# A norm's weights moved from the rows to the raw up-projection weights, and a second weight load that waits for the last row norm

## The chip, the cores and the metric

One core of one Trainium2 chip runs the whole kernel. The metric is the device time of one execution in microseconds. A time is compared with a run of the kernel before on the same chip.

## What is computed

One layer of a decoder trunk on 1024 tokens of width 1024, in float32. The first half of the layer (a norm, one input projection, pooling heads and differential attention, one output projection with a residual add) is not touched. What matters is the second half, cut from the reference:

```
h  = rms_norm(x, norm_ffn_g[l], NORM_EPS)        # x * rsqrt(mean(x*x) + eps) * g, row by row
gu = h @ ffn_w_in[l]                             # 1024 -> 2 * 2816
g  = causal_depthwise_conv(gu[..., :D_FF], ffn_conv_w[l], ffn_conv_b[l])
u  = gu[..., D_FF:]
x  = x + (jax.nn.silu(g) * u) @ ffn_w_out[l]     # 2816 -> 1024
return rms_norm(x, norm_final_g, NORM_EPS)
```

## The kernel before, in words

Every product in float32 is made of three products of values split into a high part (a cast by ScalarE) and a low part (a subtraction by VectorE or GpSimd): L79 and L80 for weights, L83 and L84 for activations. TensorE (PE in the profile) is busy nearly throughout.

**The output projection and the second norm.** `out_rows` (L538 to L541) adds the last three groups of the output projection to the eight row tiles x1 of 128 tokens, tile by tile, two halves of 512 columns each. Behind each tile `norm2` squares the two halves on ScalarE (L566), stores the tile to memory (L568, on ScalarE's DMA queue), makes the reciprocal root with small steps on VectorE, ScalarE and VectorE (L570 to L576, and L108, L109, L111 of `newton`), and scales the tile with one VectorE instruction that multiplies by the row's factor and by the norm's weights g_ffn (L577). The tile is scaled where it lies, so L577 waits until the store of the unscaled tile has left.

**The blocks.** The up-projection is a fast 2x2 block product with seven products in place of eight. Its token operands are seven blocks: b11, b21 (the two halves of an even tile), b22 (the second half of an odd tile) and t1 to t4, sums of halves of an even and an odd tile made by `pair_blocks` (L594 to L597) on GpSimd, for the last pair partly on VectorE. Each piece is transposed on TensorE into PSUM (`to_block`, L584, tiles tp_b and tp_t) and split from there by ScalarE and VectorE into h and l. A product needs its block from all four pairs.

**The weights of a channel tile.** The 2816 channels are worked through in 22 tiles ct of 128 channels. `up_weights` loads the raw weights of the u half and the g half (ru, rg, 512 KB each; one buffer for each, so the next tile's load waits until both are used up), and makes four sums: s1 and s3 on GpSimd (L628, L631), s2 and s4 on VectorE (L629, L630; s1 and s2 are the halves of sa, s3 and s4 those of sb). Then u, sa, sb and a quarter of g (gt) are split: uh, ul, sah, sal, sbh, sbl. `ffn_up` runs seven products of 12 matmuls each (L650; 84 for a tile, 1848 in all) in the order 1 6 7 5 2 4 3, with steps between them that empty a bank: product 1 uses uh, ul and b11; product 6 sah, sal and t2; product 7 sbh, sbl and t3; product 5 sah, sal and t1; product 2 uh, ul and b21; product 4 gt and t4; product 3 sbh, sbl and b22. After product 5 ScalarE copies a bank into eb (L674), and products 3 and 4 can't start until that copy, and VectorE's add behind it (L675), are done.

**The order.** A scheduler fixes each engine's order when the kernel is built, mixing products of neighbouring channel tiles; on the chip every engine works through its own list in that order, and the head of a list blocks what is behind it. So the lists below are facts of the build, and only the times in them come from the chip.

Of the kernel before, what the change touches and what calls it, by code (L numbers as in the profile page):

```python
# [9 lines left out]
F32 = mybir.dt.float32  # L10
F32R = mybir.dt.float32r
AF = mybir.ActivationFunctionType
ALU = mybir.AluOpType
PSUM = bass.MemoryType.PSUM

P = 128
S = 1024
D = 1024
KC = D // P
NT = S // P  # L20
# [22 lines left out]
def trunk_kernel(ctx, tc, x, norm_mix_g, w_in, pool_w, rows, line, rel_bias, w_out, norm_ffn_g,  # L43
                 ffn_w_in, ffn_w_out, norm_final_g, onehot, out):
    nc = tc.nc
# [7 lines left out]
    const = ctx.enter_context(tc.tile_pool(name="const", bufs=1))  # L53
# [5 lines left out]
    att = st_att.enter_context(tc.tile_pool(name="att", bufs=1))  # L59
# [5 lines left out]
    def sc_ps(name):  # L65
        return ps_a.tile([P, 512], F32, tag="sc", bufs=3, name=name)

    def pv_ps(name):
        return ps_a.tile([P, 512], F32, tag="pv", bufs=1, name=name)
# [8 lines left out]
    def split(hi, lo, src, lo_eng=None):  # L78
        nc.scalar.copy(hi, src)  # L79
        (lo_eng or nc.gpsimd).tensor_tensor(lo, src, hi.bitcast(F32), op=ALU.subtract)  # L80
# [33 lines left out]
    def row_rstd(src, sq, name):  # L114
        ss = small.tile([P, 1], F32, tag="ss", name=f"ss_{name}")
        nc.scalar.activation(sq, src, AF.Square, accum_out=ss)
        var = small.tile([P, 1], F32, tag="var", name=f"var_{name}")
        nc.vector.tensor_scalar(var, ss, 1.0 / D, EPS, op0=ALU.mult, op1=ALU.add)
        r = small.tile([P, 1], F32, tag="rs", name=f"rs_{name}")
        lg = small.tile([P, 1], F32, tag="lg", name=f"lg_{name}")  # L120
        nc.scalar.activation(lg, var, AF.Ln)
        nc.scalar.activation(r, lg, AF.Exp, scale=-0.5)
        return newton(r, var, name)
# [25 lines left out]
    ident = const.tile([P, P], F32, name="ident")  # L149
# [20 lines left out]
        return xt  # L170


    prow = att.tile([96, P], F32, tag="ln", bufs=2, name="prow")
    flat = att.tile([P, 276], F32, tag="hank", bufs=1, name="flat")
    lam_in = flat[:, 0:256].rearrange("p (j c) -> p j c", c=64)
    recfar = const.tile([P, 20], F32, name="recfar")
# [4 lines left out]
    def load_params():  # L181
        nc.vector.memset(rb[32:33, :], NEG)
        nc.sync.dma_start(rb[0:32, :], rel_bias)
        nc.sync.dma_start(oh, onehot)
        nc.sync.dma_start(flat, line.to_broadcast((P, 276)))
        nc.sync.dma_start(prow[0:93, :], rows)

    prm = const.tile([P, 96], F32, name="prm")
    gsub = const.tile([P, 1], F32, name="gsub")
    nlam = const.tile([P, 1], F32, name="nlam")  # L190

    def small_params():
        r_ps = sc_ps("r_ps")
        nc.tensor.matmul(r_ps[0:NH, :], rb, oh, start=True, stop=True)
        r_sb = att.tile([NH, 512], F32, tag="vt", bufs=1, name="r_sb")
        nc.vector.tensor_copy(r_sb, r_ps[0:NH, :])
        nc.sync.dma_start(scratch, r_sb)
        prm_ps = sc_ps("prm_ps")
        nc.tensor.transpose(prm_ps[:, 0:93], prow[0:93, :], ident[0:93, 0:93])
        nc.vector.tensor_copy(prm[:, 0:93], prm_ps[:, 0:93])  # L200
        nc.vector.tensor_scalar(gsub, prm[:, 92:93], 1.0 - LAM_INIT, None, op0=ALU.mult)
        nc.vector.tensor_copy(recfar, flat[:, 256:276])
        lam_s = const.tile([P, 2], F32, name="lam_s")
        lam_p = att.tile([P, 64], F32, tag="tb", bufs=1, name="lam_p")
        for j in range(2):
            nc.vector.tensor_tensor_reduce(lam_p, lam_in[:, 2 * j, :], lam_in[:, 2 * j + 1, :], 1.0, 0.0,
                                           ALU.mult, ALU.add, lam_s[:, j:j + 1])
        lam_e = const.tile([P, 2], F32, name="lam_e")
        nc.scalar.activation(lam_e, lam_s, AF.Exp)
        nc.vector.tensor_tensor(nlam, lam_e[:, 1:2], lam_e[:, 0:1], op=ALU.subtract)  # L210
        nc.vector.tensor_scalar(nlam, nlam, -LAM_INIT, None, op0=ALU.add)
# [109 lines left out]
    for t in range(NT):  # L321
# [8 lines left out]
        xt = xs[t]  # L330
        sq = att.tile([P, S], F32, tag="pl", bufs=3, name=f"sq_{t}")
        r = row_rstd(xt, sq, f"m{t}")
# [184 lines left out]
    mid = ctx.enter_context(tc.tile_pool(name="mid", bufs=2, side="right"))  # L517

    def u_tile(dt, name):
        return wide.tile([P, S], dt, tag="u", name=name)  # L520

    def x_tile(dt, name):
        return wide.tile([P, S], dt, tag="x", bufs=4, name=name)
# [4 lines left out]
    x1 = [None] * NT  # L528
# [16 lines left out]
    for s in OUT_PLAN.split():  # L545
        if s[0] == "w":
            wo[int(s[1])] = out_weights(int(s[1]))
        else:
            out_rows(int(s[1]), wo[int(s[1])], int(s[2]))
    g_bc2 = mid.tile([P, D], F32, tag="gt", bufs=1, name="g_ffn")  # L550
    nc.sync.dma_start(g_bc2, norm_ffn_g.to_broadcast((P, D)))
    st_ws.close()
    st_slots.close()

# [6 lines left out]
    def norm2(t):  # L561
        xt = x1[t]
        ss = small.tile([P, 2], F32, tag="ss2", name=f"ssf_{t}")
        junk = pv_ps(f"junk_{t}")
        for half in range(2):
            nc.scalar.activation(junk, xt[:, half * 512:half * 512 + 512], AF.Square,  # L566
                                 accum_out=ss[:, half:half + 1])
        nc.scalar.dma_start(x1_d[t * P:(t + 1) * P, :], xt)  # L568
        var = small.tile([P, 1], F32, tag="var", name=f"varf_{t}")
        nc.vector.tensor_scalar(var, ss[:, 0:1], 1.0 / D, EPS, op0=ALU.mult, op1=ALU.add)  # L570
        nc.vector.tensor_scalar(var, ss[:, 1:2], 1.0 / D, var, op0=ALU.mult, op1=ALU.add)
        r = small.tile([P, 1], F32, tag="rs", name=f"rsf_{t}")
        lg = small.tile([P, 1], F32, tag="lg", name=f"lgf_{t}")
        nc.scalar.activation(lg, var, AF.Ln)
        nc.scalar.activation(r, lg, AF.Exp, scale=-0.5)
        r = newton(r, var, f"f{t}")  # L576
        nc.vector.scalar_tensor_tensor(xt, xt, r, g_bc2, op0=ALU.mult, op1=ALU.mult)  # L577

    def to_block(src, b, j):
        tp = (sc_ps if b[0] == "t" else tp_ps)(f"tp_{b}_{j}")  # L580
# [35 lines left out]
    def up_weights(ct):  # L616
        raw = []
        for n, c in (("u", NCT + ct), ("g", ct)):
            r = mid.tile([P, KC * P], F32, tag="rw", bufs=2, name=f"r{n}{ct}")
            src = ffn_w_in[:, c * P:(c + 1) * P].rearrange("(k p) c -> p k c", p=P)  # L620
            nc.sync.dma_start(r.rearrange("p (k c) -> p k c", c=P), src)
            raw.append(r)
        u, g = raw
        a11, a12, a21, a22 = u[:, 0:512], u[:, 512:1024], g[:, 0:512], g[:, 512:1024]
        sa = mid.tile([P, S], F32, tag="st", bufs=2, name=f"sa{ct}")
        sb = mid.tile([P, S], F32, tag="st", bufs=2, name=f"sb{ct}")
        s1, s2, s3, s4 = sa[:, 0:512], sa[:, 512:1024], sb[:, 0:512], sb[:, 512:1024]
        nc.gpsimd.tensor_tensor(s1, a21, a22, op=ALU.add)  # L628
        nc.vector.tensor_tensor(s2, s1, a11, op=ALU.subtract)  # L629
        nc.vector.tensor_tensor(s4, a12, s2, op=ALU.subtract)  # L630
        nc.gpsimd.tensor_tensor(s3, a11, a21, op=ALU.subtract)  # L631
        uh, ul = u_tile(F32R, f"uh{ct}"), u_tile(F32R, f"ul{ct}")
        split(uh, ul, u)
        gt = x_tile(F32R, f"gt{ct}")
        split(gt[:, 0:512], gt[:, 512:1024], a22, nc.vector)
        sh = []
        for n, t in (("a", sa), ("b", sb)):
            h, l = (u_tile if n == "a" else x_tile)(F32R, f"s{n}h{ct}"), u_tile(F32R, f"s{n}l{ct}")
            split(h, l, t, nc.vector)
            sh.append((blocks(h), blocks(l)))  # L640
        (ah, al), (bh_, bl_), (uh, ul), gb = sh[0], sh[1], (blocks(uh), blocks(ul)), blocks(gt)
        return {"1": (uh[:, 0], ul[:, 0], "b11"), "2": (uh[:, 1], ul[:, 1], "b21"), "3": (bh_[:, 1], bl_[:, 1], "b22"),
                "4": (gb[:, 0], gb[:, 1], "t4"), "5": (ah[:, 0], al[:, 0], "t1"), "6": (ah[:, 1], al[:, 1], "t2"),
                "7": (bh_[:, 0], bl_[:, 0], "t3")}
# [112 lines left out]
    ct = 0  # L757
    for gi, n in enumerate(DOWN):
        ops = []
        for c in range(ct, ct + n):  # L760
            rows = slice(c * P, (c + 1) * P)
# [31 lines left out]
def _arrays(a):  # L793
    import numpy as np
    onehot, rec = _tables()
    a = {n: np.asarray(v) for n, v in a.items()}
    rows = np.concatenate([a[n].reshape(-1, P) for n in ('ffn_conv_w', 'ffn_conv_b', 'pool_scale', 'subln_g')])
    line = np.concatenate([a[n].reshape(1, -1) for n in ('lambda_q1', 'lambda_k1', 'lambda_q2', 'lambda_k2')]
                          + [rec, a['rel_bias'][31:32]], axis=1)
    return [('x', a['x']), ('norm_mix_g', a['norm_mix_g']), ('w_in', a['w_in']), ('pool_w', a['pool_w']),  # L800
            ('rows', rows), ('line', line), ('rel_bias', a['rel_bias']), ('w_out', a['w_out']),
            ('norm_ffn_g', a['norm_ffn_g']), ('ffn_w_in', a['ffn_w_in']), ('ffn_w_out', a['ffn_w_out']),
            ('norm_final_g', a['norm_final_g']), ('onehot', onehot)]
# [22 lines left out]
```

## Time and profile before

| | |
|---|---|
| median of 3 runs | 1113.54 us (1113.4 to 1116.36) |
| the profiled execution's own time | 1115.49 us |
| its span in the trace | 1113.7 us |
| up-projection products, first to last start | 429.02 to some 866 us |
| mean granted TensorE clock, as a share of full speed | 0.987 |

The span is what the trace shows of the profiled execution; 1.8 us of its own time lie around it. Busy shares are averages over stages with different limits. The stage that the change touches is the passage from the output projection to the up-projection, at about 390 to 490 us, and the 22 channel tiles behind it, up to about 850 us.

### The profile page before, as it was taken

The numbers are of one execution on the slowest core, as the hardware profiler recorded it, in microseconds if no ns is written. First come the engines' busy times: TensorE is split into PE (matmuls) and PEld (weight loads), VectorE is DVE, ScalarE is ACT, GpSimd is POOL, SyncE is SP. The second block draws the span as 40 slices with busy tenths as digits, with TensorE's granted clock in tenths as the row PEclk, the third lists the DMA queues.
The fourth block names the chain that finished last, engine by engine and source line by source line (L and its number), as shares of the span: only waits on it lengthen the run. The fifth ranks groups of instructions, "written<-read, shape, count | busy, mean of one in ns | idle before, by whom it ended". The sixth has DMA issues, their size and how long they took to land.

```text
span 1113.7 us, 13597 instructions
## 1 busy us (share of the span) xinstructions
PE 1066.6 (96%) x5011; PEld 884.0 (79%) x5011; DVE 732.3 (66%) x1213; ACT 475.9 (43%) x775; POOL 341.7 (31%) x240
## 2 busy tenths in 40 slices
PE   5999999999899997999999999999999999999997
PEld 4988888887677675878888888888888788888885
DVE  7556787877797689577657656755665655544545
ACT  5557476655752355244333443443344222111133
POOL 3232242433730247133312232221314322221211
PEclk9999999999899998999999999999999999999999
DMA  8010110110386742123122212222247632212112
GB/s 242 28 50 27 43 46 19 43 39 26 133 278 216 242 171 76 57 95 95 57 94 95 93 59 96 90 81 76 82 127 267 223 114 99 89 60 95 39 50 102
DMA packets 85990, 111.76 MB, mean 100 GB/s; under 512 B 3618, under 2 KB 66303, under 8 KB 85924
## 3 DMA queue, kind: packets, MB, share of 16 engines
q1 hardware_dynamic: 79300, 86.78, 24.4%
q10 hardware_dynamic: 6624, 24.12, 5.5%
q8 instruction: 39, 0.64, 0.2%
q14 instruction: 27, 0.22, 0.1%
HBM read 82.57 MB, written 28.32 MB: 100 GB/s over the span
## 4 chain that ended last, share of the span: by engine, by line
PE 81%; DVE 8%; issue 4%; DMA 3%; ACT 1%; POOL 1%; SPq 1%; DVEq 0%; ACTq 0%; POOLq 0%
PE p L650 36%; PE fo L747 7%; PE fo L749 7%; PE fo L748 7%; PE tpa L402 1%; PE z_q L144 1%; PE z_q L145 1%; PE z_q L143 1%; PE o L538 1%; PE o L539 1%; PE o L540 1%; PE z_p L143 1%; PE z_p L144 1%; PE z_p L145 1%; PE z_v L143 1%
## 5 line engine op out<-in xcount | busy, mean ns | idle before, releaser
L747 PE MATMUL fo<-w,a 128*128 128x512 f32 x352 | 137.3, 390 | 2.8 <-DVE xr L750 2.8
L750 DVE TENSOR_TENSOR xr<-xr,fo 128x512 f32<-128x512 f32 x112 | 75.9, 684 | 97.0 <-PE fo L749 96.3
L748 PE MATMUL fo<-w,a 128*128 128x512 f32 x352 | 137.0, 389 | 0.0
L749 PE MATMUL fo<-w,a 128*128 128x512 f32 x352 | 137.0, 389 | 0.0
L80 POOL TENSOR_TENSOR w<-rw,w 128x1024 fp32r<-128x1024 f32 x22 | 61.3, 2796 | 156.4 <-ACT w L79 151.1
L628 POOL TENSOR_TENSOR sa<-rg 128x512 f32<-128x512 f32 x22 | 32.9, 1495 | 209.8 <-DMA rg<-in_ffn_w_in_dram 201.3
L80 POOL TENSOR_TENSOR ul<-ru,uh 128x1024 fp32r<-128x1024 f32 x22 | 58.1, 2642 | 71.8 <-PE p L650 37.6
L747 PEld LDWEIGHTS fo<-w,a 128*128 128x128 f32 x352 | 66.1, 188 | 17.6 <-DVE xr L750 4.0
L749 PEld LDWEIGHTS fo<-w,a 128*128 128x128 f32 x352 | 66.1, 188 | 13.9
L748 PEld LDWEIGHTS fo<-w,a 128*128 128x128 f32 x352 | 66.1, 188 | 13.6
L79 ACT CAST a<-ra 128x1024 fp32r<-128x1024 f32 x22 | 23.1, 1051 | 118.8 <-DVE xr L750 64.1
L362 ACT ACTIVATE p<-p,nm 128x128 f32<-128x128 f32 (+7 forms) x64 | 49.6, 776 | 40.9 <-DVE nm L361 40.5
L650 PE MATMUL p<-t4h,gt 128*128 128x512 f32 x176 | 58.9, 396 | 1.7 <-DVE g L675 1.7
L629 DVE TENSOR_TENSOR sa<-sa,ru 128x512 f32<-128x512 f32 x22 | 39.9, 1814 | 21.1 <-POOL sa L628 21.1
L538 PE MATMUL o<-woh,yh 128*128 128x512 f32 x128 | 51.9, 409 | 1.6 <-DVE x L541 1.4
L349 POOL CAST qz<-q 64x128 fp32r<-64x128 f32 x64 | 24.5, 384 | 92.3 <-PE s L353 85.4
L79 ACT CAST uh<-ru 128x1024 fp32r<-128x1024 f32 x22 | 23.2, 1054 | 68.0 <-PE p L650 67.4
L539 PE MATMUL o<-wol,yh 128*128 128x512 f32 x128 | 50.6, 397 | 1.4 <-POOL wol L80 1.4
L677 DVE TENSOR_TENSOR g<-eb,p 128x512 f32<-128x512 f32 x22 | 15.1, 687 | 55.5 <-PE p L650 55.5
L80 DVE TENSOR_TENSOR a<-ra,a 128x1024 fp32r<-128x1024 f32 x22 | 43.0, 1956 | 12.1 <-ACT a L79 11.6
L540 PE MATMUL o<-woh,yl 128*128 128x512 f32 x128 | 50.0, 393 | 0.9 <-DVE yl L80 0.9
L79 ACT CAST gt<-rg 128x512 fp32r<-128x512 f32 x22 | 13.7, 623 | 82.1 <-PE p L650 75.1
(264 smaller groups left out, 3111.0 us busy)
## 6 DMA issues: line engine op xcount, KB each, us to landing
x_rows<-x ACTq DMA_DIRECT2D x24, 512.0 KB, 3.6
ru<-in_ffn_w_in_dram SPq DMA_DIRECT2D x22, 512.0 KB, 4.0
rg<-in_ffn_w_in_dram SPq DMA_DIRECT2D x22, 512.0 KB, 3.9
act_rows<-cv ACTq DMA_DIRECT2D x22, 512.0 KB, 2.6
rw<-in_ffn_w_out_dram SPq DMA_DIRECT2D x22, 512.0 KB, 4.4
ra<-act_rows SPq DMA_DIRECT2D x22, 512.0 KB, 3.4
x<-in_x_dram SPq DMA_DIRECT2D x16, 512.0 KB, 5.6
x<-x_rows SPq DMA_DIRECT2D x16, 512.0 KB, 3.7
```

What stands on the lines that cost most here:

```text
L79: nc.scalar.copy(hi, src)
L80: (lo_eng or nc.gpsimd).tensor_tensor(lo, src, hi.bitcast(F32), op=ALU.subtract)
L362: nc.scalar.activation(s[:, 0:w], s[:, 0:w], AF.Exp, bias=negm[:, c:c + 1], accum_out=sums[:, c:c + 1])
L538: nc.tensor.matmul(ps, yh[:, ts], wh[:, cs], start=n == 0, stop=False)
L539: nc.tensor.matmul(ps, yh[:, ts], wl[:, cs], start=False, stop=False)
L540: nc.tensor.matmul(ps, yl[:, ts], wh[:, cs], start=False, stop=n == len(wo) - 1)
L629: nc.vector.tensor_tensor(s2, s1, a11, op=ALU.subtract)
L650: nc.tensor.matmul(ps, w[:, k, :], h[:, k, :], start=start and k == 0 and n == 0, stop=k == 3 and n == 2, skip_group_check=not start)
L747: nc.tensor.matmul(ps, ah[:, ts], wh[:, cs], start=n == 0, stop=False)
L748: nc.tensor.matmul(ps, ah[:, ts], wl[:, cs], start=False, stop=False)
L749: nc.tensor.matmul(ps, al[:, ts], wh[:, cs], start=False, stop=n == len(ops) - 1)
L750: nc.vector.tensor_tensor(xr[t][:, cs], xr[t][:, cs], ps, op=ALU.add)
```

## The change

The norm's weights norm_ffn_g are no longer multiplied into the rows. They arrive with the other small parameters (eight more rows of a table that is transposed once, so that prm[:, 93:101] holds the weight of input channel k*128+p in partition p, column k), and the broadcast load of g_ffn is gone. Two GpSimd instructions for each channel tile multiply the raw weights ru and rg by them, in place, before the sums. A row tile is scaled by its factor alone, on ScalarE. For channel tile 1 a one-column VectorE copy from the last scaled row tile writes into each raw buffer first, so that this tile's loads wait until the last row norm is done.

```
-    g_bc2 = mid.tile([P, D], F32, tag="gt", bufs=1, name="g_ffn")
-    nc.sync.dma_start(g_bc2, norm_ffn_g.to_broadcast((P, D)))
...
         r = newton(r, var, f"f{t}")
-        nc.vector.scalar_tensor_tensor(xt, xt, r, g_bc2, op0=ALU.mult, op1=ALU.mult)
+        nc.scalar.mul(xt, xt, r)
...
             r = mid.tile([P, KC * P], F32, tag="rw", bufs=2, name=f"r{n}{ct}")
+            if ct == 1:
+                nc.vector.tensor_copy(r[:, 0:1], x1[NT - 1][:, D - 1:D])
             src = ffn_w_in[:, c * P:(c + 1) * P].rearrange("(k p) c -> p k c", p=P)
             nc.sync.dma_start(r.rearrange("p (k c) -> p k c", c=P), src)
+            r3 = r.rearrange("p (k c) -> p k c", c=P)
+            nc.gpsimd.tensor_tensor(r3, r3, prm[:, 93:101].unsqueeze(2).to_broadcast((P, KC, P)), op=ALU.mult)
             raw.append(r)
```

The lines of the changed kernel stand two lower or two to three higher than those before: `pair_blocks` is L592 to L595, s1 to s4 are L630 to L633, the new multiplication is L623, the row scaling on ScalarE L575, the new copies L619, products L652.

**GpSimd, at the third pair of row tiles.** In these lists x1_2_5 is row tile 5, ta2 and tb2 hold the sums of pair 2, and the digit behind ru, rg, uh, ul, sa, sb is the channel tile. Before:

```order
L80 TENSOR_TENSOR ul0_4513<-ru0_4502,uh0_4512 128x1024
L628 TENSOR_TENSOR sa0_4506<-rg0_4504 128x512
L594 TENSOR_TENSOR ta2_4322<-x1_2_5_4280,x1_2_4_4224 128x512
L595 TENSOR_TENSOR tb2_4323<-x1_2_5_4280 128x512
L631 TENSOR_TENSOR sb0_4507<-ru0_4502,rg0_4504 128x512
L596 TENSOR_TENSOR ta2_4322<-x1_2_5_4280,ta2_4322 128x512
L597 TENSOR_TENSOR tb2_4323<-x1_2_4_4224,ta2_4322 128x512
L595 TENSOR_TENSOR tb3_4462<-x1_2_7_4419 128x512
```

and in the changed kernel:

```order
L592 TENSOR_TENSOR ta2_4320<-x1_2_5_4278,x1_2_4_4222 128x512
L593 TENSOR_TENSOR tb2_4321<-x1_2_5_4278 128x512
L594 TENSOR_TENSOR ta2_4320<-x1_2_5_4278,ta2_4320 128x512
L80 TENSOR_TENSOR ul0_4513<-ru0_4500,uh0_4512 128x1024
L630 TENSOR_TENSOR sa0_4506<-rg0_4503 128x512
L633 TENSOR_TENSOR sb0_4507<-ru0_4500,rg0_4503 128x512
L595 TENSOR_TENSOR tb2_4321<-x1_2_4_4222,ta2_4320 128x512
L593 TENSOR_TENSOR tb3_4460<-x1_2_7_4417 128x512
L623 TENSOR_TENSOR ru1_4527<-ru1_4527,prm_104 128x1024
L623 TENSOR_TENSOR rg1_4531<-rg1_4531,prm_104 128x1024
L80 TENSOR_TENSOR ul1_4542<-ru1_4527,uh1_4541 128x1024
L630 TENSOR_TENSOR sa1_4535<-rg1_4531 128x512
```

Channel tile 0's ul and s1 moved behind three sums of pair 2, and the two multiplications of channel tile 1 stand ahead of its ul and s1.

**VectorE, at the last row norm.** rt_f7 and rr_f7 are the last small steps of row tile 7's norm. Before:

```order
L629 TENSOR_TENSOR sa0_4506<-sa0_4506,ru0_4502 128x512
L630 TENSOR_TENSOR sb0_4507<-ru0_4502,sa0_4506 128x512
L84 TENSOR_TENSOR b11l_3939<-tp_b11_3_4405,b11h_3932 128x4x128
L108 TENSOR_SCALAR rt_f7_4455<-varf_7_4448,rsf_7_4451 128x1
L80 TENSOR_TENSOR sal0_4520<-sa0_4506,sah0_4519 128x1024
L109 TENSOR_SCALAR rt_f7_4455<-rt_f7_4455 128x1
L84 TENSOR_TENSOR b21l_3940<-tp_b21_3_4412,b21h_3933 128x4x128
L84 TENSOR_TENSOR t1l_3942<-tp_t1_2_4335,t1h_3935 128x4x128
L111 TENSOR_SCALAR rr_f7_4458<-rsf_7_4451,rt_f7_4455 128x1
L84 TENSOR_TENSOR t3l_3944<-tp_t3_2_4342,t3h_3937 128x4x128
L577 SCALAR_TENSOR_TENSOR x1_2_7_4419<-x1_2_7_4419,rr_f7_4458,g_ffn_3925 128x1024
```

and in the changed kernel:

```order
L631 TENSOR_TENSOR sa0_4506<-sa0_4506,ru0_4500 128x512
L84 TENSOR_TENSOR t3l_3942<-tp_t3_2_4340,t3h_3935 128x4x128
L84 TENSOR_TENSOR t2l_3941<-tp_t2_2_4347,t2h_3934 128x4x128
L632 TENSOR_TENSOR sb0_4507<-ru0_4500,sa0_4506 128x512
L84 TENSOR_TENSOR b11l_3937<-tp_b11_3_4403,b11h_3930 128x4x128
L84 TENSOR_TENSOR b21l_3938<-tp_b21_3_4410,b21h_3931 128x4x128
L80 TENSOR_TENSOR sal0_4520<-sa0_4506,sah0_4519 128x1024
L108 TENSOR_SCALAR rt_f7_4453<-varf_7_4446,rsf_7_4449 128x1
L80 TENSOR_TENSOR sbl0_4524<-sb0_4507,sbh0_4523 128x1024
L84 TENSOR_TENSOR t4l_3943<-tp_t4_2_4354,t4h_3936 128x4x128
L109 TENSOR_SCALAR rt_f7_4453<-rt_f7_4453 128x1
L111 TENSOR_SCALAR rr_f7_4456<-rsf_7_4449,rt_f7_4453 128x1
```

The scaling of the row tile is gone from this list, and the step that releases it (L111) moved from behind seven instructions after s2 (L629) to behind ten (after L631). Behind it come the first sum of pair 3 (L592) and then the two copies (L619) that hold the second weight load.

**ScalarE, at channel tile 3.** uh3 is the cast of channel tile 3's raw weights, eb1 the copy after product 5 of channel tile 1. Before:

```order
L674 COPY eb1_4685<-p6_1_4682 128x512
L79 CAST gt2_4670<-rg2_4658 128x512
L679 ACTIVATE cv0_4558<-g0_4557,prm_104 128x1024
L79 CAST sbh2_4677<-sb2_4661 128x1024
L79 CAST uh3_4795<-ru3_4785 128x1024
```

and in the changed kernel:

```order
L79 CAST gt2_4676<-rg2_4663 128x512
L681 ACTIVATE cv0_4562<-g0_4561,prm_104 128x1024
L79 CAST sbh2_4683<-sb2_4667 128x1024
L79 CAST uh3_4803<-ru3_4791 128x1024
L676 COPY eb1_4691<-p6_1_4688 128x512
```

The copy eb1 moved behind the cast uh3, which needs channel tile 3's raw weights multiplied.

## Rows read from the trace of the kernel before

**Rows 1.** Profile page, part 1: busy time, share of the span, instructions.

```profile
PE 1066.6 (96%) x5011; PEld 884.0 (79%) x5011; DVE 732.3 (66%) x1213; ACT 475.9 (43%) x775; POOL 341.7 (31%) x240
```

**Rows 2.** Busy time by stretch; columns: stretch, length, engines, granted clock, DMA share, GB/s.

```profile
391.10:422.70 31.60, 30.25 (x165) 25.42 (x165) 28.71 (x61) 18.32 (x51) 11.45 (x9) 1.00 0.47 167
422.70:448.00 25.30, 18.85 (x81) 14.29 (x80) 24.79 (x31) 12.05 (x23) 20.04 (x11) 0.80 0.20 64
...
480.00:490.20 10.20, 8.46 (x30) 6.50 (x29) 8.32 (x9) 3.82 (x4) 3.53 (x2) 0.83 0.49 154
...
580.00:599.10 19.10, 19.10 (x86) 15.82 (x85) 13.00 (x13) 7.47 (x9) 5.35 (x3) 1.00 0.22 65
```

**Rows 3.** Timeline of PE: start, length, instruction, idle time before and its releaser.

```profile
392.06 1.09 PE L584 MATMUL tp_b<-ident,x 128*128 128x128 f32 x8 [0.77 <-DVE x L577]
...
407.12 0.50 PE L538 MATMUL o<-woh,yh 128*128 128x512 f32 x1 [0.58 <-DVE x L541]
...
422.66 0.60 PE L584 MATMUL tp_b<-ident,x 128*128 128x128 f32 x4
425.99 1.63 PE L584 MATMUL tp_b<-ident,x 128*128 128x128 f32 x8 [2.73 <-DVE x L577]
...
429.02 0.78 PE L650 MATMUL p<-b11h,uh 128*128 128x512 f32 x1
...
443.19 0.75 PE L584 MATMUL tp_t<-ident,tb 128*128 128x128 f32 x4 [2.49 <-DVE t2l L84]
...
483.04 0.50 PE L650 MATMUL p<-t4h,gt 128*128 128x512 f32 x1 [1.74 <-DVE g L675]
...
487.97 0.40 PE L650 MATMUL p<-b11h,ul 128*128 128x512 f32 x1
...
490.24 0.39 PE L650 MATMUL p<-t2h,sah 128*128 128x512 f32 x1
```

**Rows 4.** The chain of waits, two merged pieces: start, length, what.

```profile
404.36 0.44 PE tp_t L584 x4
...
483.04 369.03 PE p L650 x1619
```

**Rows 5.** Instructions of L577: count, ns min/median/max, first and last start.

```profile
L577 DVE SCALAR_TENSOR_TENSOR x<-x,rr_f,g_ffn x8: 1274/1286/1932, 390.7 to 434.5; 128x1024 f32<-128x1024 f32 x8
```

**Rows 6.** Instructions of L732, a ScalarE scaling by a column: same columns.

```profile
L732 ACT ACTIVATE o<-xg,rr_l x4: 1135/1136/1137, 1072.2 to 1104.9; 128x1024 f32<-128x1024 f32 x4
```

**Rows 7.** GpSimd's two-input instructions, same columns.

```profile
L718 POOL TENSOR_TENSOR xg<-xr,g_fin x4: 2388/2392/2399, 1068.9 to 1101.6; 128x1024 f32<-128x1024 f32 x4
...
L80 POOL TENSOR_TENSOR ul<-ru,uh x18: 2402/2635/2865, 500.9 to 819.7; 128x1024 fp32r<-128x1024 f32 x18
...
L628 POOL TENSOR_TENSOR sa<-rg x22: 1285/1423/2254, 424.7 to 817.2; 128x512 f32<-128x512 f32 x22
...
L631 POOL TENSOR_TENSOR sb<-ru,rg x18: 1280/1288/2269, 492.1 to 818.5; 128x512 f32<-128x512 f32 x18
```

**Rows 8.** VectorE's and ScalarE's instructions on the weights, same columns.

```profile
L629 DVE TENSOR_TENSOR sa<-sa,ru x18: 1755/1763/1777, 493.1 to 818.6; 128x512 f32<-128x512 f32 x18
L630 DVE TENSOR_TENSOR sb<-ru,sa x18: 676/693/2305, 495.0 to 820.9; 128x512 f32<-128x512 f32 x18
L79 ACT CAST uh<-ru x18: 1051/1051/1059, 499.7 to 816.7; 128x1024 fp32r<-128x1024 f32 x18
...
L80 DVE TENSOR_TENSOR sal<-sa,sah x18: 1211/1506/2109, 502.3 to 824.3; 128x1024 fp32r<-128x1024 f32 x18
```

**Rows 9.** Profile page, part 6: the raw weight loads, KB, median us to landing.

```profile
ru<-in_ffn_w_in_dram SPq DMA_DIRECT2D x22, 512.0 KB, 4.0
```

**Rows 10.** Timelines of GpSimd and VectorE around 479 us, columns as in rows 3.

```profile
438.73 3.16 POOL L80 TENSOR_TENSOR ul<-ru,uh 128x1024 fp32r<-128x1024 f32 x1 [0.73 <-ACT uh L79]
...
479.00 2.84 POOL L80 TENSOR_TENSOR ul<-ru,uh 128x1024 fp32r<-128x1024 f32 x1
...
479.51 2.88 DVE L629 TENSOR_TENSOR sa<-sa,ru 128x512 f32<-128x512 f32 x1
```

More of the change, by code (lines that the diff above doesn't have):

```diff
@@ L170, in load_x @@
         return xt
-    prow = att.tile([96, P], F32, tag="ln", bufs=2, name="prow")
+    prow = att.tile([104, P], F32, tag="ln", bufs=2, name="prow")
     flat = att.tile([P, 276], F32, tag="hank", bufs=1, name="flat")
@@ L185, in load_params @@
         nc.sync.dma_start(flat, line.to_broadcast((P, 276)))
-        nc.sync.dma_start(prow[0:93, :], rows)
-    prm = const.tile([P, 96], F32, name="prm")
+        nc.sync.dma_start(prow[0:101, :], rows)
+    prm = const.tile([P, 104], F32, name="prm")
     gsub = const.tile([P, 1], F32, name="gsub")
@@ L198, in small_params @@
         prm_ps = sc_ps("prm_ps")
-        nc.tensor.transpose(prm_ps[:, 0:93], prow[0:93, :], ident[0:93, 0:93])
-        nc.vector.tensor_copy(prm[:, 0:93], prm_ps[:, 0:93])
+        nc.tensor.transpose(prm_ps[:, 0:101], prow[0:101, :], ident[0:101, 0:101])
+        nc.vector.tensor_copy(prm[:, 0:101], prm_ps[:, 0:101])
         nc.vector.tensor_scalar(gsub, prm[:, 92:93], 1.0 - LAM_INIT, None, op0=ALU.mult)
@@ L796, in _arrays @@
     a = {n: np.asarray(v) for n, v in a.items()}
-    rows = np.concatenate([a[n].reshape(-1, P) for n in ('ffn_conv_w', 'ffn_conv_b', 'pool_scale', 'subln_g')])
+    rows = np.concatenate([a[n].reshape(-1, P) for n in ('ffn_conv_w', 'ffn_conv_b', 'pool_scale', 'subln_g',
+                                                            'norm_ffn_g')])
     line = np.concatenate([a[n].reshape(1, -1) for n in ('lambda_q1', 'lambda_k1', 'lambda_q2', 'lambda_k2')]
```

## The prediction

> **What bounds the kernel now.** The page's first part says TensorE: busy 96% of the span, VectorE 66%, GpSimd 31% [rows 1]. But that is an average, so I read busy time by stretch next [rows 2]. There the reader is to see two kernels. In a stretch of the length of one channel tile at 580 us TensorE is busy for all of 19.10 us at the full clock, beside 13.00 us of VectorE and 5.35 us of GpSimd. In the passage (422.70 to 448) TensorE is busy for 18.85 us of 25.30 at a granted clock of 0.80, while VectorE is busy for 24.79. Then TensorE's timeline [rows 3], for what it waited for there: 2.73 us for L577's scaling of a row tile, 2.49 us for a split by VectorE, and at 483.04 another 1.74 us. Last the chain of waits [rows 4]: from 483.04 it is 1619 matmuls in 369.03 us, 0.228 us for each, nothing else. So any gain or loss is made before 490, and the steady part matters only if it stops being bound by TensorE.
>
> How much there is to win can be read off. In the passage's list the matmul at 490.24 is number 204 of the up-projection, counted from zero, in the order of before as in that of the change, and the first 204 are the same work in both. From 422.66, where the output projection's matmuls are done, to there lie 204 matmuls of 0.228 us (46.5) and twelve groups of four transposes of 0.44 us (5.3) [rows 4]: 51.8 us of work in 67.6. 15.8 us are lost, to idle time and to the lower clock behind it. After the stall at 483.04 fourteen matmuls took until 487.97, 4.93 us in place of 3.19: a stall of under 2 us costs 1.7 more in clock. The whole prediction is the time at which the changed kernel reaches matmul 204.
>
> **The change, part by part.**
>
> *L577 leaves VectorE.* Eight instructions of 1.27 to 1.93 us, median 1.29 [rows 5], 10.3 us or more off the engine that is busy 28.71 us of 31.60 while the tiles come by [rows 2]. ScalarE takes eight scalings of 1.14 us, the price of the same operation at L732 [rows 6]: 9.1 us on top of 18.32 in those 31.60, which fits. With the load of g_ffn gone the store that holds up the first scaling has less traffic beside it. I take it that the waits of 0.77 and 0.58 us [rows 3] go, so the output projection ends at 422.66 - 1.35 = 421.3. Left alone, they would cost 1.35.
>
> *The parameters* (eight more rows of a table, transposed once) cost nothing that can be seen: the same load and the same transpose, at the start.
>
> *The multiplications, steady.* A channel tile gets two of 128x1024. No row shows one with a broadcast operand. Below stands the same operation with a full second operand and no company, 2.39 us (L718); above, ul beside a busy VectorE, up to 2.87 and once 3.16 [rows 7, 10]. I take 2.6, near ul's median, as the place is ul's own. GpSimd goes from 5.35 to 10.6 us of 19.1. Because there is one buffer for ru and one for rg, a cycle is: issue 0.4, load 4.0 [rows 9], two multiplications 5.2, ul 2.6, s1 1.4, s3 1.3 [rows 7], VectorE's s4 behind it some 1.4: 16.3 us, under 19.1. So 0 us in the steady part; the cover is TensorE's own 84 matmuls, and it is gone if one multiplication takes over 4.0 us.
>
> A rule speaks against this change. The row: at 479.51 VectorE's s2 took 2.88 us, against 0.69 for a 128x512 operation alone (the median of L630, rows 8), while GpSimd ran ul for 2.84 [rows 8, 10]. The Trainium skill, GPSIMD Engine Reference, sections 4.1 and 8, says that elementwise work belongs on VectorE, since GpSimd is about half as fast with two inputs, and that GpSimd shares its SBUF interfaces with VectorE, so that VectorE's instructions with two SBUF inputs collide with it. The trace agrees with the collision. Taken at its worst the rule would have VectorE stand still for all of the added 5.2 us, 18.2 of 19.1 us busy, still no loss in the steady part; what it does in the passage is the slower rival below.
>
> *The passage, step by step* (estimates, from the durations of rows 5 to 9 and the lists of the changed kernel). Half 0 of row tile 6 leaves TensorE 27 matmuls and three groups of transposes ahead of 421.3: 413.8. Behind its add and square (some 2.4 us) row tile 5's factor is ready, and ScalarE has scaled tile 5 at 417.4. GpSimd then does three sums of pair 2 (1.3 to 2.3 each, 1.5 taken), ul 2.6 and s1 1.5, all in its list ahead of s2: 426.0. This is where the stall goes: VectorE's list has row tile 7's last steps behind s2 (1.76), s4 and the five splits t3l, t2l, b11l, b21l and t4l at 0.69 each (4.1), sal 1.5, sbl 1.2 and three small steps (0.6): 435.2. ScalarE scales tile 7 by 436.3; before it was scaled by 436.2 at the latest (L577's last start 434.5 and 1.7). So VectorE's 10 us buy nothing here: its wait for GpSimd takes their place.
>
> Late next is the second weight load. Its copies stand behind that scaling and a sum of pair 3 (1.4): 438.0 with the copies. Issue and load 4.4: 442.4. Two multiplications 447.6, ul 450.3, s1 451.8, s2 453.5, the cast sah 454.6, and some 0.6 for eight handovers: **455.2**. What is queued behind the load: on SP only the later weight loads, on GpSimd nothing but this chain.
>
> TensorE needs this sah at its matmul 60. Left to itself, it has after tile 7's scaling (436.3) 48 matmuls (10.9), five groups of transposes (2.2), and 1.7 of lower clock: 451.1. So it waits some 4 us. From 455.2 it is 144 matmuls to number 204 (32.8), and 1.7 for the clock behind the wait: 489.7. One more wait may lie between: product 3 of channel tile 1 starts at matmul 162 (480.1), and needs eb1, which now stands behind uh3 on ScalarE. Channel tile 3's ru goes through two more cycles of 16.3 less what its own later steps take: s4 of tile 1 at 454.9, load 459.3, two multiplications, ul, s1, s3 and s4 471.2, load 475.6, multiplication 478.2, uh3 1.1, eb1 0.6: 479.9. It just fits; I add 0.5.
>
> **Sum.** 490.2 against 490.24: the three stalls of before (with their clock 15.8 us) give way to about as much waiting for the chain GpSimd, VectorE, ScalarE, load, GpSimd. Span 1113.7 + 0. The profiled execution's own time, 1115.49, is 1.95 above the median of the runs shown; against the median 1113.54 I predict 1114, the half microsecond for the steps that I may have missed.
>
> **The rivals.** *Faster.* The same chain with short instructions: s2 0.69 and sal 1.2 as VectorE has them alone, GpSimd's sums 1.3, ul 2.4, multiplications 2.39, load 3.8. Tile 7 is scaled 2.2 us sooner and sah1 4.7 us sooner (450.5); then little is left of the wait, and TensorE is at matmul 204 some 5 us sooner: 1109. For it: VectorE did lose 10 us of work. Against: GpSimd is busy 20.04 of 25.30 us already [rows 2], so short instructions are few there. TensorE's own 451.1, less the 2.2, sets the limit: no better than 1107.
>
> *Slower, by the collision.* GpSimd's two multiplications and VectorE's two-input operations stretch each other, as in rows 10: 3.16 in place of 2.6. Five multiplications and two ul lie ahead of eb1: 2.8 + 0.8 us, and a stall there that draws 1.7 of clock: 5.3 us, 1119. It decides from about 3.1 us for a multiplication; below that the loss stays under 3.3. For it: 3.16 has been seen in this very place. Against: the median is 2.64. The page's rule above is this rival's.
>
> *The broadcast is dear.* An operand read with stride 0 in eight pieces could run at half speed, 4.8 us: five times 2.2 in the passage (11), and in the steady part a cycle of 20.7 against 19.1, 20 to 30 us more: 1135 to 1145. Nothing in the trace speaks for it or against it.
>
> **How the numbers follow.** 0.42 for my forecast, 0.27 faster, 0.24 for the collision, 0.07 for the dear broadcast. 0.3% (3.3 us) is about what a measurement of this kernel can tell from no change, so the chances are 0.27, 0.42 and 0.31. The range reaches from 1108 (leaving out the last of the faster case) to 1121 (leaving out the dear broadcast and a little of the collision). As cases of both signs hold most of the chance: the likeliest one's own range is 1110.5 to 1116.5.
>
> **What would show it right or wrong.** L623 at 2.4 to 2.9 us each; L575 at 1.14. Matmul 204, the first with channel tile 3's sah, at 490, with TensorE's longest wait ahead of it at channel tile 1's sah or ul, at about 451 to 455, and none worth a microsecond from 500 to 850. VectorE's s2 of channel tile 0 at about 426, waiting for GpSimd, and row tile 7 scaled at about 436. I am wrong if tile 7 is scaled by 433 (then faster), if L623 is over 3.1 us (then slower), or if TensorE waits in the steady part.

## The result, and the profile after

| | before | after |
|---|---|---|
| median | 1114.08 us (4 runs, 1113.4 to 1116.36) | 1126.32 us (4 runs, 1125.12 to 1128.77) |
| ratio, 95% interval | | 1.0115 [1.0099, 1.0131] |
| the profiled execution's span | 1113.7 us | 1123.4 us |

The changed kernel is 1.15% slower, some 12 us. Forecast were 1114 us, within 1108 to 1121, and no difference to speak of.

The page's first part (it answers to [rows 1]):

```profile
PE 1078.2 (96%) x5011; PEld 879.8 (78%) x5011; DVE 725.2 (65%) x1207; ACT 483.6 (43%) x783; POOL 434.7 (39%) x284
```

GpSimd has 93 us more to do, as meant. But TensorE, with the same 5011 instructions, is busy for 11.6 us more. The span is 9.7 us longer: TensorE waits less than before, and is busy for longer by more than that saves.

Busy time in the stretches of [rows 2], same columns:

```profile
391.10:422.70 31.60, 31.16 (x173) 26.05 (x172) 20.38 (x53) 22.81 (x56) 12.01 (x10) 1.00 0.49 167
422.70:448.00 25.30, 19.20 (x86) 14.07 (x85) 19.06 (x33) 15.26 (x27) 15.67 (x10) 0.87 0.21 63
480.00:490.20 10.20, 10.20 (x46) 8.18 (x45) 9.00 (x9) 4.24 (x5) 4.87 (x3) 1.00 0.48 154
580.00:599.10 19.10, 19.10 (x84) 15.33 (x83) 8.43 (x11) 6.49 (x8) 7.78 (x5) 1.00 0.25 83
```

In the first three TensorE is better off than before. In the last, where it was and is busy all the time at the full clock, it gets through 84 matmuls in place of 86.

TensorE's timeline in the passage: start, length, instruction, idle time before and its releaser (to [rows 3]):

```profile
431.59 1.12 PE L582 MATMUL tp_t<-ident,tb 128*128 128x128 f32 x4 [2.28 <-POOL tb L595]
...
453.73 0.50 PE L652 MATMUL p<-t2h,sah 128*128 128x512 f32 x1 [1.28 <-ACT sah L79]
...
487.55 0.39 PE L652 MATMUL p<-t2h,sah 128*128 128x512 f32 x1
...
495.79 0.50 PE L652 MATMUL p<-t1h,sah 128*128 128x512 f32 x1 [1.42 <-ACT eb L674]
```

Matmul 204 starts at 487.55, 2.7 us sooner than before; matmul 230, behind the last wait, at 495.79 against 496.14. So at 496 the changed kernel is 0.35 us ahead, and what these two executions differ by lies behind. Then comes one piece of the chain of waits (to [rows 4]):

```profile
495.79 372.20 PE p L652 x1594
```

372.20 / 1594 is 0.2335 us for each matmul. Before, the piece has 1.74 us of lower clock behind its stall (4.93 in place of 3.19), and without it (369.03 - 1.74) / 1619 = 0.2269. From 500 to 850 us no wait of TensorE is listed in either trace and the granted clock is 1.00 in both: there every matmul of the up-projection takes 0.0066 us longer. For all 1848 that would be 12.2 us, if no wait hid any of it. The down-projection's have not changed (three lines of 352 instructions, 389 or 390 ns each, in both traces; a matmul's time in the trace overlaps the next one's start). What makes a matmul slower?

### The profile page after: what moved, and what is told of

Same layout as the page of the kernel before. It is cut to its first block, busy times and chain, and to the rows that moved or that the text cites. A ratio compares the mean times of both kernels' runs of the same rounds, so it can differ in the third digit from the quotient of the medians.

```text
span 1123.4 us, 13588 instructions
## 1 busy us (share of the span) xinstructions
PE 1078.2 (96%) x5011; PEld 879.8 (78%) x5011; DVE 725.2 (65%) x1207; ACT 483.6 (43%) x783; POOL 434.7 (39%) x284
## 4 chain that ended last, share of the span: by engine, by line
PE 83%; DVE 8%; ACT 2%; issue 2%; DMA 2%; POOL 2%; SPq 1%; DVEq 0%; ACTq 0%; POOLq 0%
PE p L652 35%; PE fo L749 7%; PE fo L751 7%; PE fo L750 7%; PE o L538 1%; PE o L539 1%; PE z_q L144 1%; PE o L540 1%; PE z_q L145 1%; PE z_q L143 1%; PE z_k L144 1%; PE z_k L143 1%; PE z_k L145 1%; PE z_v L143 1%; PE tpa L402 1%
## 5 line engine op out<-in xcount | busy, mean ns | idle before, releaser
L623 POOL TENSOR_TENSOR ru<-ru,prm 128x1024 f32<-128x1024 f32 x22 | 48.8, 2220 | 99.8 <-DMA ru<-in_ffn_w_in_dram 88.2
L623 POOL TENSOR_TENSOR rg<-rg,prm 128x1024 f32<-128x1024 f32 x22 | 49.9, 2269 | 54.3 <-DMA rg<-in_ffn_w_in_dram 40.3
L80 POOL TENSOR_TENSOR ul<-ru,uh 128x1024 fp32r<-128x1024 f32 x22 | 54.9, 2495 | 34.5 <-ACT uh L79 32.0
L652 PE MATMUL p<-t4h,gt 128*128 128x512 f32 x176 | 58.9, 396 | 0.0
L79 ACT CAST sah<-sa 128x1024 fp32r<-128x1024 f32 x22 | 23.1, 1052 | 69.8 <-DVE sa L631 66.7
L631 DVE TENSOR_TENSOR sa<-sa,ru 128x512 f32<-128x512 f32 x22 | 31.2, 1416 | 30.8 <-POOL sa L630 30.8
```

Of the source, the lines that this page charges most:

```text
L623: nc.gpsimd.tensor_tensor(r3, r3, prm[:, 93:101].unsqueeze(2).to_broadcast((P, KC, P)), op=ALU.mult)
L652: nc.tensor.matmul(ps, w[:, k, :], h[:, k, :], start=start and k == 0 and n == 0, stop=k == 3 and n == 2, skip_group_check=not start)
```

## The experiments

**Theory A (placement).** The diff widens the parameter tile from 96 to 104 float32 columns, so every tile allocated behind it on the left side of SBUF moves by 32 bytes in its partition. The product blocks (b11 to t4, the moving operands of the up-projection) lie there; the weights (uh, ul, sah and so on) lie on the right side and stay. In the program's allocation of before, b11h starts at byte 20192 and uh5 at 217056. *Distance* means here the start of the moving operand less the start of the weights: before it is a multiple of 256 (-769 x 256). After, they are at 20224 and 221152, and the distance is 32 more than a multiple (-785 x 256 + 32). All slices of the blocks lie a multiple of 2048 bytes apart, all weight slices 512, so modulo 256 all 1848 matmuls have the one distance. The down-projection has both operands on the left, and its distance stays. **Theory B (traffic):** GpSimd's added reads and writes of SBUF slow TensorE. **Theory C:** the values of the weights, or something in the changed instructions.

**e1, the kernel before with the tile widened alone; e2 and e3, the changed kernel with a wider tile yet; e4, the kernel before with the right side moved.** The edits:

```diff
-    prm = const.tile([P, 96], F32, name="prm")
+    prm = const.tile([P, 104], F32, name="prm")     # e1
-    prm = const.tile([P, 104], F32, name="prm")
+    prm = const.tile([P, 128], F32, name="prm")     # e2; 112 in e3
+    edge = ctx.enter_context(tc.tile_pool(name="edge", bufs=1, side="right"))   # e4
+    edge_t = edge.tile([P, 8], F32, name="edge_t")
     wide = ctx.enter_context(tc.tile_pool(name="wide", bufs=10, side="right"))
```

> The kernel before, with nothing changed but the width of the parameter tile (96 to 104 float32 columns, the added ones unused): every tile allocated behind it on the left side moves by 32 bytes in each partition, those on the right side stay; every instruction is the same. Theory A (placement): a matmul runs slower where its moving operand and its weights lie 32 bytes apart modulo 64; then the up-projection's matmuls start every 0.2335 us in place of 0.2279, 1848 of them, about 10 us, and with the in-projection's 1125 us (1123 to 1128). Theory B (GpSimd's added SBUF traffic slows TensorE) and theory C (the values of the weights, or something else in the changed instructions): no change, 1114.

> The changed kernel with the parameter tile 128 columns wide: everything on the left side lies where it lay before, modulo 128 bytes, and the instructions are those of the changed kernel. Theory A: the matmuls of the up-projection go back to 0.2279 us; 1126.3 less 1848 x 0.0056 (10.3) and 0 to 2 in the in-projection: 1114 to 1116. What is left against the kernel before is the price of the change itself. Theories B and C: 1126.

> The changed kernel with the parameter tile 112 columns wide: moving operand and weights of the up-projection have the same address modulo 64 bytes but lie 64 apart modulo 128. If theory A's period is 64 bytes: the same as with 128 columns, 1114 to 1116. If it is 128 bytes: slow, or in between, 1120 to 1126. Theories B and C: 1126.

> The kernel before with an unused tile of 8 float32 columns at the edge of the right side, so that the weights of the up-projection move by 32 bytes and its moving operand stays. Theory A, and that only the distance counts: the up-projection at 0.2335 us, the in- and the down-projection as before: 1114 + 10.3 = 1124. If it is the place of the moving operand that counts (slow at a multiple of 64): no change, 1114. Theories B and C: 1114.

Measured: e1 1124.54 us, ratio to before 1.0110 [1.0093, 1.0126]; e2 1125.19, 1.0111 [1.0093, 1.0128]; e3 1120.14, 1.0065 [1.0045, 1.0084]; e4 1124.61, 1.0108 [1.0089, 1.0127]. The steady piece of the chain, of e1:

```profile
485.56 375.48 PE p L650 x1608
```

Of e4:

```profile
483.06 375.48 PE p L652 x1608
```

Of e2:

```profile
495.92 370.68 PE p L652 x1594
```

Of e3:

```profile
498.59 365.17 PE p L652 x1594
```

e1 and e4 give 0.2335 us for a matmul, as the changed kernel has, with none of its instructions. e1 moves the moving operand and e4 the weights; in both the distance becomes 32 modulo 256, and the pace is the same to the last digit. That speaks for A, and that the distance counts and not the place of either operand. But e2 missed: 0.2326, where I had expected the old pace (I wrote 0.2279, the whole piece of before with its lower clock; 0.2269 is the figure to compare). e3, at 0.2291, is the in-between of the second of its two cases, but that case, a period of 128, asked for the old pace in e2. Either the period is longer than 128, or B holds as well.

**e5, the left side back at the old addresses; e6, the distance of e2 in the kernel before; e7, e5 without the multiplications (norm_ffn_g is then left out of the result); e8, e5 without the wait of the second load.**

```diff
-    gsub = const.tile([P, 1], F32, name="gsub")     # e5, in the changed kernel
-    nlam = const.tile([P, 1], F32, name="nlam")
+    gn = const.tile([P, 2], F32, name="gn")
+    gsub, nlam = gn[:, 0:1], gn[:, 1:2]
-    prm = const.tile([P, 96], F32, name="prm")      # e6, in the kernel before
+    prm = const.tile([P, 128], F32, name="prm")
-            nc.gpsimd.tensor_tensor(r3, r3, prm[:, 93:101].unsqueeze(2).to_broadcast((P, KC, P)), op=ALU.mult)  # e7, in e5
-            if ct == 1:                             # e8, in e5, with the line behind it
-                nc.vector.tensor_copy(r[:, 0:1], x1[NT - 1][:, D - 1:D])
```

> The changed kernel with gsub and nlam in one tile of two columns (they had a 32-byte place each), which takes back the 32 bytes that the wider parameter tile adds: every tile behind it lies at exactly the address of the kernel before. Theory A, sharpened by the first four runs: the pace of a matmul hangs on the distance between the start of its moving operand and that of its weights, modulo 256 bytes (0: 0.2267 us, 32: 0.2333, 64: 0.2288, 128: 0.2324), in whatever kernel. Then 0.2267 us in the up-projection and 1848 x 0.0066 = 12.2 us less than the changed kernel: 1113 to 1115. Rival B: the change's own traffic slows TensorE as well, which is why widths 128 and 112 did not bring back the old pace: 0.229 to 0.2325 us, 1118 to 1125.

> The kernel before with the parameter tile 128 columns wide: distance 128 modulo 256, no other change. Theory A: 0.2324 us in the up-projection, as the changed kernel had at this distance, and 1113 + 10.5 = 1123 to 1125. Rival B: 0.2267 us and 1113.

> The kernel of e5 without the 44 multiplications on GpSimd; so norm_ffn_g is left out of the result, all else stays. It prices the multiplications at the old addresses. Theory A: 0.2267 us as in e5, and in the passage the 3.8 us of two multiplications leave the chain to channel tile 1's sums, so the waits of 1.28 and 1.4 us go: 2 to 4 us less than e5. Rival B: the pace comes back only here: e5 less 4 to 12 us.

> The kernel of e5 without the two copies that let the second weight load wait for row tile 7's scaling. The load then waits only until channel tile 0's ru and rg are read (about 432 in place of 438.7): its data, and so the multiplications and sums, come some 5 us sooner, channel tile 1's sah before TensorE wants it, and the waits of 1.28 and 1.4 us go: 2 to 4 us less than e5. Rival: the load collides with the last stores and the row tile's own chain, tile 7 is scaled later, and the time is that of e5 or up to 3 us more.

Measured: e5 1114.99 us, ratio 1.0019 [1.0004, 1.0033] over 12 runs; e6 1122.06 (one run); e7 1113.32, 1.0002 [0.9986, 1.0018]; e8 1118.82, 1.0045 [1.0027, 1.0064]. The steady piece of e5:

```profile
494.25 362.45 PE p L652 x1594
```

Of e6:

```profile
482.64 373.95 PE p L650 x1608
```

Of e7:

```profile
483.06 373.04 PE p L651 x1644
```

e5 has all the changed instructions and 0.2274 us for a matmul (some 0.7 us of the piece are short waits); it takes back 11.3 of the 12 us. Where they lie can be read from the two traces, one execution each. At the last matmul of the output projection e5 is 1.6 us ahead of the changed kernel (420.22 against 421.84), at matmul 230 of the up-projection still 1.5 (494.25 against 495.79), and the piece behind is 9.75 us shorter. So the slower pace costs some 1.6 us ahead of the up-projection, and nothing in its first 230 matmuls: e5 waits there for what the changed kernel's slower matmuls just cover. At matmul 60 it waits longer (1.28 us in the changed kernel), and at 476.85 where the changed kernel doesn't:

```profile
452.24 0.50 PE L652 MATMUL p<-t2h,sah 128*128 128x512 f32 x1 [1.41 <-ACT sah L79]
...
476.85 0.50 PE L652 MATMUL p<-t4h,gt 128*128 128x512 f32 x1 [0.49 <-DVE g L677]
```

e6 has GpSimd's old list, and at the distance of e2 it has the pace of e2, 0.2326. e6 is one run, and its time a microsecond under what was expected; its pace is what counts. So A stands with the modulus 256, and B and C fall: with the multiplications or without, the pace is that of the distance. The change itself costs 1.5 us of median against before (0.04 to 0.33%). Without the multiplications it is 1.7 us less; the two intervals overlap, so that this is a hint that they are what it costs, and no proof.

e8 went the wrong way: 3.8 us more than e5 by the medians, 2.9 by the two ratios, whose intervals touch; in the profiled executions it is 2.4 us behind e5 at matmul 230. VectorE's list in e8, the same columns as TensorE's:

```profile
433.16 2.73 DVE L80 TENSOR_TENSOR sbl<-sb,sbh 128x1024 fp32r<-128x1024 f32 x1
...
438.09 2.46 DVE L592 TENSOR_TENSOR ta<-x,x 128x512 f32<-128x512 f32 x1 [1.28 <-ACT x L575]
...
442.77 1.18 DVE L595 TENSOR_TENSOR tb<-x,ta 128x512 f32<-128x512 f32 x1
443.86 1.76 DVE L629 TENSOR_TENSOR sa<-sa,ru 128x512 f32<-128x512 f32 x1
445.66 0.69 DVE L630 TENSOR_TENSOR sb<-ru,sa 128x512 f32<-128x512 f32 x1
446.27 0.69 DVE L80 TENSOR_TENSOR gt<-rg,gt 128x512 fp32r<-128x512 f32 x1
446.87 1.22 DVE L80 TENSOR_TENSOR sal<-sa,sah 128x1024 fp32r<-128x1024 f32 x1
448.00 0.68 DVE L84 TENSOR_TENSOR t1l<-tp_t,t1h 128x512 fp32r<-128x512 f32 x1
```

and what TensorE waits for:

```profile
448.74 1.12 PE L582 MATMUL tp_t<-ident,tb 128*128 128x128 f32 x4 [2.52 <-DVE t1l L84]
```

The load does come sooner, and its sums with it; but they now stand ahead of row tile 7's split t1l (441.18 in e5, 448.00 here), for which TensorE waits 2.5 us. Besides, GpSimd's multiplications now fall into row tile 7's norm: sbl takes 2.73 us beside them, where it takes 1.21 in e5, so that the tile is scaled 1.5 us later, and the sum behind it takes 2.46 beside GpSimd's ul in place of 0.69. The rival was right that tile 7 is scaled later and that the time grows, but not by the transfers: by the order on VectorE and by what runs beside it on GpSimd. How much each of the two costs is not separated.

**e9, e5 with the gate half first; e10, the kernel before at distance 96; e11, e5 with the row scaling on VectorE.**

```diff
-        for n, c in (("u", NCT + ct), ("g", ct)):   # e9, in e5
+        for n, c in (("g", ct), ("u", NCT + ct)):
-        u, g = raw
+        g, u = raw
-    prm = const.tile([P, 96], F32, name="prm")      # e10, in the kernel before
+    prm = const.tile([P, 120], F32, name="prm")
-        nc.scalar.mul(xt, xt, r)                    # e11, in e5
+        nc.vector.tensor_scalar(xt, xt, r, None, op0=ALU.mult)
```

> The kernel of e5 with the gate half of each channel tile's weights loaded and multiplied ahead of the up half. The first sum (s1) needs the gate half alone, so GpSimd's list becomes rg, ru, s1, s3, ul in place of ru, rg, ul, s1, s3, and channel tile 1's sah comes some 2.4 us sooner. If the chain through GpSimd to that sah is what the passage waits for: the waits of 1.41 us at matmul 60 and, behind it, of 0.49, 0.62 and 1.41 go in part, 1.4 to 3.9 us less than e5, 1111 to 1113.5. Rival: ul, now last, or VectorE's sbl and eb become what TensorE waits for, and the time is that of e5, 1115.

> The kernel before with the parameter tile 120 columns wide: distance 96 modulo 256, no other change. One more point of theory A's curve (0: 0.2267 us, 32: 0.2333, 64: 0.2288, 128: 0.2324). If what counts is whether the distance is an odd multiple of 32: 0.2333 as at 32, and 1125. If the pace falls off with the distance from 0: between 0.2288 and 0.2324, 1117 to 1123. Rival B: 0.2267.

> The kernel of e5 with the row scaling back on VectorE (without the weights, which GpSimd still applies). The prediction held that taking it off VectorE buys nothing in the passage, since VectorE's wait for GpSimd takes its place. By that: within 1.5 us of e5, 1113.5 to 1116.5. Rival: VectorE's list is what makes row tile 7 late, each scaling in it counts: 2 to 5 us more than e5, 1117 to 1120.

Measured: e9 1117.58 us, ratio 1.0034 [1.0021, 1.0048]; e10 1125.67 (one run); e11 1117.35, 1.0030 [1.0020, 1.0040]. TensorE's waits in e9:

```profile
454.98 0.50 PE L652 MATMUL p<-t2h,sah 128*128 128x512 f32 x1 [2.41 <-ACT sah L79]
...
457.80 0.79 PE L652 MATMUL p<-t3h,sbh 128*128 128x512 f32 x1 [2.09 <-ACT sbh L79]
```

And VectorE's two sums ahead of them, in e9:

```profile
452.10 1.75 DVE L631 TENSOR_TENSOR sa<-sa,ru 128x512 f32<-128x512 f32 x1 [0.58 <-POOL sa L630]
453.88 2.73 DVE L632 TENSOR_TENSOR sb<-ru,sa 128x512 f32<-128x512 f32 x1
```

From the start of row tile 7's scaling to s2 it is 12.7 us in e9 (439.38 to 452.10) and 14.05 in e5 (435.30 to 449.35). The chain is shorter by 1.3 us, not 2.4: the up half now lands last, and GpSimd waits 0.62 us for it ahead of s1; and s4, which took 0.68 us in e5, takes 2.73 beside GpSimd's ul. A miss: no gain. (The profiled execution of e9 took 1122.06 us; its granted clock was 0.95 from 200 to 400 us, where e5 had 0.98, so only differences inside the passage are read from it.) e11 lies 2.4 us above e5 by the medians, just inside what the rival expected, and 1.2 us by the two ratios, inside what I did; the intervals overlap. That is not decided.

e10's piece:

```profile
484.51 375.48 PE p L650 x1608
```

0.2335 us again, as at 32, in the mean of all products (more on this at the end).

**e12, the kernel before with the identity moved to distance 0 of what it transposes.**

```diff
+    recfar = const.tile([P, 20], F32, name="recfar")
     ident = const.tile([P, P], F32, name="ident")
...
-    recfar = const.tile([P, 20], F32, name="recfar")
```

> The kernel before with one small tile of constants allocated ahead of the identity instead of behind it: the identity moves by 96 bytes, everything behind it stays where it was. The 368 transposes, whose two operands lie 160 bytes apart modulo 256 in the kernel before (as the 16 sums of squares, at 96), then lie at distance 0 like all other matmuls there. Theory A, if it holds for 128 columns too: four transposes in a row take less than the 0.44 us of before, by up to 0.02 or 0.03, and the time falls by up to 2 us, 1111 to 1113. Rival: at 128 columns the distance does not count, 0.44 us and no change, 1113.

Measured: 1113.08 us, ratio 1.0002 [0.9992, 1.0012]. Four transposes start 0.44 us ahead of what follows them, as before, so the distance does not show at 128 columns. Of the other matmuls of the kernel before all but some 20 (16 of them the sums of squares) lie at distance 0 already, and in e12 those do too: there was nothing left to win there. No version beat the kernel before.

## Why the prediction was wrong

**The step that failed** is the shortest: "*The parameters* (eight more rows of a table, transposed once) cost nothing that can be seen". I had counted their load and their transpose, and not the 32 bytes that they take. With that went "0 us in the steady part": I had checked whether TensorE would wait there, and had taken its 0.228 us for granted, because its instructions are the same. It did not wait, and each matmul took 0.2335 us in place of 0.2269: 10.5 us for the 1594 behind matmul 230. No rival of mine had it. e1 shows the loss with this one edit, e5 takes it away by undoing its shift alone. "I am wrong if TensorE waits in the steady part" was too narrow as well.

**The sum otherwise held.** At the old addresses the change is worth 1114.99 us; forecast were 1114, and 1110.5 to 1116.5 as the likeliest case's own range. That it came so near is in part luck, since misses of opposite sign cancel in it: matmul 204 came sooner than forecast (by 4 us in e5), and a wait behind it, which no term has, took 2.5 us of that back (from matmul 204 to 230 it is 8.4 us in e5, 5.9 in before). Its steps, in the trace of after:

- *The multiplications*: 2.6 us taken, 1.99 and 2.16 measured (medians). So the dear broadcast is out, and so is the threshold of 3.1. What ScalarE's scaling takes was right (1.14, measured 1.15). Both groups: count, ns min/median/max, first and last start.

```profile
L623 POOL TENSOR_TENSOR ru<-ru,prm x22: 1902/1987/2891, 383.0 to 819.2; 128x1024 f32<-128x1024 f32 x22
L623 POOL TENSOR_TENSOR rg<-rg,prm x22: 1898/2158/2879, 387.3 to 826.5; 128x1024 f32<-128x1024 f32 x22
...
L575 ACT ACTIVATE x<-x,rr_f x8: 1133/1152/1160, 389.8 to 436.8; 128x1024 f32<-128x1024 f32 x8
```

- *The chain of the second load*: GpSimd's list shows it whole.

```profile
442.99 1.90 POOL L623 TENSOR_TENSOR ru<-ru,prm 128x1024 f32<-128x1024 f32 x1 [3.09 <-DMA ru<-in_ffn_w_in_dram]
444.85 1.90 POOL L623 TENSOR_TENSOR rg<-rg,prm 128x1024 f32<-128x1024 f32 x1
446.70 2.40 POOL L80 TENSOR_TENSOR ul<-ru,uh 128x1024 fp32r<-128x1024 f32 x1
449.06 1.74 POOL L630 TENSOR_TENSOR sa<-rg 128x512 f32<-128x512 f32 x1
```

Row tile 7 was scaled from 436.80 to 437.95 (forecast 436.3), the load was there at 442.9 (442.4), the sah came at 453.7 (455.2), and matmul 60 waited 1.28 us (4). The chain was right in kind and order, and each of its times within 1.7 us. But it was not TensorE's longest wait, as I had written: that was 2.28 us at 431.59, for GpSimd's last sum of pair 2 (tb), which stands behind ul, s1 and s3 in its list.

- *Row tile 5* was forecast to be scaled by 417.4 and was by 420.7, and channel tile 0's s2 started at 428.7 in place of 426.0. The store still held it, as ScalarE's timeline shows; I had let that wait go with the load of g_ffn, without a row for it:

```profile
419.56 1.15 ACT L575 ACTIVATE x<-x,rr_f 128x1024 f32<-128x1024 f32 x1 [2.37 <-DMA x_rows<-x]
```

- *Matmul 204* came at 487.55 (forecast 489.7 to 490.2), and at 485.83 in e5. But I had stopped counting there, and the passage had not ended: 26 matmuls on stands the wait of 1.42 us for eb at 495.79. VectorE's list ahead of it:

```profile
488.35 2.92 DVE L80 TENSOR_TENSOR sbl<-sb,sbh 128x1024 fp32r<-128x1024 f32 x1
491.19 2.92 DVE L684 SCALAR_TENSOR_TENSOR cv<-g,prm,cv 128x1022 f32<-128x1022 f32 x1
```

At 455.14 the same sbl took 1.23 us; here GpSimd's two multiplications run beside it (487.61 and 490.52, 2.58 and 2.51 us each). Without the multiplications, in e7, the same two are short, and no wait follows at matmul 230 (e7's last wait is one of 2.02 us at 483.06, where before has its 1.74):

```profile
487.24 1.23 DVE L80 TENSOR_TENSOR sbl<-sb,sbh 128x1024 fp32r<-128x1024 f32 x1 [0.44 <-ACT sbh L79]
...
490.19 1.28 DVE L683 SCALAR_TENSOR_TENSOR cv<-g,prm,cv 128x1022 f32<-128x1022 f32 x1
```

Behind cv stand ScalarE's silu and its copy eb. This is the collision of the second rival, in small: from matmul 204 to 230 the changed kernel gives back 2.3 of the 2.7 us won, most of it in this wait and in one of 0.34 us for sbl. The Trainium skill, GPSIMD Engine Reference, section 8, has VectorE's instructions with two SBUF inputs collide with GpSimd; this row agrees.

- *VectorE's 10 us buy nothing*: e11 puts 1.2 to 2.4 us on them, by ratios or medians, with intervals that overlap. Not settled.

That e5's profiled execution has a span 1.6 us under that of before, and its median is 1.5 us above, is no contradiction: single executions of e5 lie between 1112.74 and 1119.64.

## What to carry to other kernels

When a kernel is slower, first divide a stretch in which the bound engine never waits by its instructions, before and after; only then look for waits. An edit that changes the size of a tile moves every tile behind it, however small it is: compare the addresses of both matmul operands in the two built programs, and pack small tiles so that the old distance comes back. A result with moved addresses says nothing of the edit that moved them until the addresses are put back.

## What the runs showed of the hardware

In these runs TensorE's time for a matmul of 128x512 in float32r hangs on the distance in bytes within a partition, the start of its moving operand less that of its weights, modulo 256. From the steady piece of the up-projection at the full granted clock, the mean of all products:

| distance modulo 256 | us for each matmul | kernels |
|---|---|---|
| 0 | 0.2269 to 0.2274 | before, e5, e7 |
| 32 | 0.2335 | after, e1, e4 |
| 64 | 0.2291 | e3 |
| 96 | 0.2335 | e10 |
| 128 | 0.2326 | e2, e6 |

It is the same in kernels with and without GpSimd's added work, and whichever operand was moved. Modulo 512 the up-projection of before lies at 256 and the down-projection at 0, at one pace (0.227 us from start to start), so 0 and 256 count as the same; 64 and 128 don't count as 0. So 256 is the smallest power of two that fits as a period.

The in-projection goes the same way. Its moving operand (hTh) lies on the right and its weights (whi) on the left, so that a wider parameter tile lowers its distance by as much as it raises the up-projection's. Its 512-column matmuls (L143 to L145) start every 0.227 us (median at the full clock) in before, e4 and e5, whose left side lies in the old place at that time, and every 0.233 in after, e1 and e3. So in e3 the in-projection, at 64 less than a multiple, is slower than the up-projection at 64 more (0.2291): the direction counts.

The distance is not the whole rule. From 520 to 850 us every product of after takes 395 ns and every one of before 389 or 390, but at 96 and at 64 the products differ at one distance. In e10 (count, busy us, mean ns, idle time before):

```profile
L650 PE MATMUL p<-t2h,sah 128*128 128x512 f32 x68 | 27.1, 399 | 0.0
...
L650 PE MATMUL p<-t2l,sah 128*128 128x512 f32 x68 | 26.7, 392 | 0.0
```

and in e3:

```profile
L652 PE MATMUL p<-t2l,sah 128*128 128x512 f32 x69 | 26.8, 388 | 0.0
L652 PE MATMUL p<-t2h,sah 128*128 128x512 f32 x68 | 26.8, 394 | 0.0
```

So that 32 and 96 have one mean doesn't make them one case. Why the distance counts, these runs don't show. Transposes of 128 columns didn't react.
